# A two-layer recurrent decoder trunk: moving the small tiles so that the large ones start on multiples of 256 bytes

## The chip, the cores and the metric

The kernel runs on one core of a Trainium2 chip. The metric is the time of one execution on the device in microseconds (us), as the median of several runs; less is better. TensorE (PE in the profile) multiplies matrices, VectorE (DVE), ScalarE (ACT) and GpSimd (POOL) work elementwise, and SyncE (SP) issues all of this kernel's transfers. The on-chip memory has 128 partitions; a tile takes the same range of byte addresses in each of them, and that range is what this change moves.

## What is computed

The input x has 512 tokens of 2048 float32 values. Two layers and a last norm follow:

```
x = x + lru_mlstm_layer(rmsnorm(x, e_norm), ...)     # layer 0
x = x + ssd_layer(rmsnorm(x, o_norm), ...)           # layer 1
return rmsnorm(x, final_norm)

def lru_mlstm_layer(x, w_in, ...):
    u = x @ w_in                                     # 2048 -> 8192
    x_l, x_m, z = split(u)
    y_l = rglru(causal_conv(x_l), ...)               # gated linear recurrence
    q, k, v, o = projections of conv(x_m) and x_m    # 4 heads
    y_m = o * rmsnorm(mlstm_chunkwise(q, k, v, gates))
    return (concat(y_l, y_m) * silu(z)) @ w_out      # 4096 -> 2048

def ssd_layer(x, w_in, ...):
    z, xbc, dt = split(x @ w_in)                     # 2048 -> 10304
    y = ssd_scan(silu(causal_conv(xbc)), softplus(dt + dt_bias), ...)
    return rmsnorm_by_group(y * silu(z)) @ w_out     # 4096 -> 2048
```

All arrays are float32. About nine tenths of the arithmetic is the four large products with `w_in` and `w_out`.

## The kernel before

Everything lies transposed: channels on the partitions, the 512 tokens along the free dimension. A float32 product is made of three products in a faster format (`fp32r` in the profile): a value is split into a high and a low part, and `mm3` (lines 136 to 140) issues high by high (L138), high weight by low activation (L139) and low weight by high activation (L140). Each is a 128x128 weight tile (the stationary operand, loaded by LDWEIGHTS, `PEld` in the profile) against a 128x512 activation tile (the moving operand).

- `acc` holds the running x, 16 tiles of 128x512. `prenorm` writes its two parts, multiplied by the norm's weights, into `xh[0..15]` and `xl[0..15]`. Every input projection of both layers (`proj`) has these as its moving operands: in the profile `xm`, `zm`, `xl`, `zl`, `xbc`, `z` and `dt` name the results, and the operands read `xh,whi`, `xl,whi` and `xh,wlo`.
- `load_w` brings weights: one DMA of 128x1024 into `wraw` (2 buffers), then per half a copy on ACT into `whi` (L131) and a subtraction on DVE into `wlo` (L132), 4 buffers each. Its instructions are recorded with a high priority.
- `outproj` multiplies a group's result by `w_out` and adds to `acc` (L207). Its moving operands are the working tiles `yh`, `yl` (also `ylh`, `yll`, `ymh`, `yml`); only for the last head of layer 0 and half of the last group of layer 1 do they lie in the space of `xh` and `xl`, which is free then.
- The mixers' other work (convolution, gates, attention, scan) is cut into stages, generators that `tick` moves on after a number of weight chunks, so that it fills in beside the projections. In the attention the moving operands `Ph`, `Pl` meet the stationary `vh`, `vl` (result `num`).
- At the end the 16 column tiles of the last output projection are done in two halves of 256 tokens; there the weights lie in `xh` and `xl`, as stationary operands.

The order on each engine comes from the recording order and priorities; a scheduler sets it when the program is built. The address of a tile is set by the pools: pools are stacked in the order in which they are opened, and a tile takes its bytes per partition, rounded up to 32. `prm`, the array of small parameters, is the first tile of the first pool, 872 columns or 3488 bytes, and starts 128 bytes behind a multiple of 256. Before the change the pool `cst` has behind it `eps` and `warm` (4 bytes each), `ones_r` (512), `r_bc` (2048), `acc` (32768), `xh` and `xl` (2048 each), and `raws` (2 tiles of 2060 bytes); then comes the pool `wp` with `wraw`, `whi` and `wlo`. So the distance of each start behind a multiple of 256 bytes is:

```
                          before   after
prm                         128     128
ones_r                       96       0
r_bc, acc, xh, xl            96       0
wraw, whi, wlo              160       0
raw0, raw1                96, 128   0, 32
working tiles of both
layers (yh, yl, Ph, vh,
xs, Bt, Bn, ...)            224      64
```

The working tiles' pools lie behind those of the table's first rows, and all their tiles but a few small ones are multiples of 256 bytes long, so one number holds for nearly all. Every start is a multiple of 32 before and after.

Of the kernel before, what the change touches and what calls it, by code (L numbers as in the profile page):

```python
# [9 lines left out]
F32 = mybir.dt.float32  # L10
F32R = mybir.dt.float32r
# [5 lines left out]
P = 128  # L17
# [6 lines left out]

# columns of the packed per-partition parameter array
_W = [
# [12 lines left out]
NPAR = _o  # L39
# how many weight chunks pass before each stage of the mixers' work  # L40
LAG = dict(P=6, rs=2, late=3, dtr=15, CB=5, xtr=6, st=4, yo=1, att_rs=4, vtr=2, aitr=12, num=7, pr=2)
# where the column tiles of the previous group's output projection go in
VB = (2, 2)
# [4 lines left out]
def trunk(ctx, tc, x_t, par, w_in0, w_qkvo, w_lru, w_if, w_out0, w_in1, w_out1, out):  # L48
# [4 lines left out]
    cst = ctx.enter_context(tc.tile_pool(name="cst", bufs=1))  # L53
    wp = ctx.enter_context(tc.tile_pool(name="wp", bufs=1))
    pmm = ctx.enter_context(tc.tile_pool(name="pmm", bufs=3, space=PSUM))
# [9 lines left out]
    def pc(name, j=0, n=1):  # L65
        o = OFF[name][0] + j
        return prm[:, o:o + n]
# [4 lines left out]
    v.memset(eps, EPS)  # L72
    warm = cst.tile([P, 1], F32, name="warm")
    sc.activation(warm, eps, AF.Square)
    ones_r = cst.tile([P, P], F32R, name="ones_r")
    ones = ones_r.bitcast(F32)
    r_bc = cst.tile([P, S], F32, name="r_bc")
# [4 lines left out]
    xpairs = list(zip(xh, xl))  # L82
    raws = [cst.tile([P, S + 3], F32, name=f"raw{i}") for i in range(2)]
    for t in raws:
# [6 lines left out]

# [1 line left out]
    gens = []  # L93
# [20 lines left out]

# [1 line left out]
    def load_w(src, dsts=(None, None), pieces=1, ahead=3000):  # L116
# [24 lines left out]

    # one chunk: four contraction tiles, from the k-th on, of n
    def chunk(ps, w, mov, k, n):
# [22 lines left out]

    # in pieces: a reciprocal is slow, and the weights' splits go in between
    def recip(dst, src, w=S):
        for o in range(0, w, P):
            v.reciprocal(dst[:, o:o + P], src[:, o:o + P])  # L170

    # dst = 1 / sqrt(ssq / n + eps) on all partitions; ssq: per-partition partial sums
    def rstd(dst, ssq, n):
# [9 lines left out]

    # log1p(e) for 0 <= e <= 1 as 2 atanh(e / (2 + e))
    def log1p(dst, e, t1, t2):
        v.tensor_scalar(t1, e, 2.0, None, op0=ADD)
        v.reciprocal(t1, t1)
        v.tensor_tensor(t1, e, t1, op=MUL)
        v.tensor_tensor(t2, t1, t1, op=MUL)
        v.tensor_scalar(dst, t2, 1.0 / 15, 1.0 / 13, op0=MUL, op1=ADD)  # L190
        for c in (11, 9, 7, 5, 3, 1):
            v.tensor_tensor(dst, dst, t2, op=MUL)
            v.tensor_scalar(dst, dst, 1.0 / c, None, op0=ADD)
        v.scalar_tensor_tensor(dst, t1, 2.0, dst, op0=MUL, op1=MUL)

    # softplus(s * x) for s = +-1
    def softplus(dst, x, s, t0, t1, t2):
        v.scalar_tensor_tensor(t0, x, -1.0, x, op0=MUL, op1=MAX)
        sc.activation(t0, t0, AF.Exp, scale=-1.0)
        log1p(dst, t0, t1, t2)  # L200
        v.tensor_scalar(t0, x, s, 0.0, op0=MUL, op1=MAX)
        v.tensor_tensor(dst, dst, t0, op=ADD)

    # out of PSUM, ahead of other work: the tensor engine needs the bank
    def evac(o, a, b, op):
        with tc.high_priority(offset=1000):
            v.tensor_tensor(o, a, b, op=op)  # L207

    # causal convolution of a padded tile (bias included)
    def conv(dst, raw, w, b):  # L210
# [3 lines left out]

    # the two parts of acc * norm
    def prenorm(k, norm):
# [9 lines left out]

    # acc += w_out[rows of group g].T @ y, some column tiles
    def outproj(w_out, g, ys, js, done=None):
# [9 lines left out]

    # ================= layer 0 =================
    qd = [dr.tile([2, P, S], F32, name=f"qd{h}") for h in range(NH)]  # L240
# [10 lines left out]

    nlam = L0.tile([P, 16], F32, name="nlam")
    aiT = L0.tile([P, 16], F32, name="aiT")
    ln = [L0.tile([P, 16], F32, name=f"ln{i}") for i in range(3)]

# [29 lines left out]

# [1 line left out]
    pA = tc.tile_pool(name="A", bufs=1)  # L287
# [6 lines left out]

    # four contraction tiles at a time, in the four column strips of the array
    def gate_mm(kt, rhs):
# [4 lines left out]

    # the first two column tiles go along with the loads of x
    ps01 = [mmt("xm"), mmt("xm")]
# [6 lines left out]
    for h in range(NH):  # L310
        xm, xc = [], []
        for t in range(4):
            j = 4 * h + t
            if j > 1:
                ps = mmt("xm")
                proj(ps, w_in0[16 + j], xpairs)
            else:
                ps = ps01[j]
            if j == 0:
                v.tensor_tensor(ssq0[0], ssq0[0], ssq0[1], op=ADD)  # L320
                spawn(rstd(r_bc, ssq0[0], D))
                drain()
            raw = next_raw()
            evac(raw[:, 3:], ps, r_bc, MUL)
            m = xslot("xm")
            split(m[0], m[1], raw[:, 3:])
            xm.append(m)
            a = st("ca")
            conv(a, raw, pc("cm_w", 4 * j, 4), pc("cm_b", j))
            s = st("cs")  # L330
            sc.activation(s, a, AF.Sigmoid)
            v.tensor_tensor(a, a, s, op=MUL)
            c = xslot("xc")
            split(c[0], c[1], a)
            xc.append(c)
            tick()
            if j == 0:
                # -8 softplus(-lam)
                softplus(nlam, pc("lam", 0, 16), -1.0, *ln)
                v.tensor_scalar(nlam, nlam, -8.0, None, op0=MUL)  # L340
# [64 lines left out]

    # gates of all heads: ai = i - G, M = max(0, cummax ai), exp(-m) = exp(-(G + M))
    ready = []

    def gates():
        g_s = st("gs")  # L410
        sc.copy(g_s, ps_g)
        yield 1
        pg = axt("pg")
        pe.matmul(pg[0:36], pc("gsel", 0, 36), g_s, start=True, stop=True)
        g_i, g_f, g_t0, g_t1, g_t2 = [st(f"g{i}")[0:4] for i in range(5)]
        g_G = st("gG")[0:4]
        v.tensor_scalar(g_i, pg[0:4], pc("b_i")[0:4], None, op0=ADD)
        sc.copy(g_f, pg[32:36])
        v.tensor_scalar(g_f, g_f, pc("b_f")[0:4], None, op0=ADD)
        softplus(g_G, g_f, -1.0, g_t0, g_t1, g_t2)  # L420
        for c in range(4):
            cs = slice(c * P, (c + 1) * P)
            v.tensor_tensor_scan(g_t0[:, cs], ones[0:4], g_G[:, cs],
                                 0.0 if c == 0 else g_t0[:, c * P - 1:c * P], op0=MUL, op1=ADD)
        # g_t0 = -G
        v.tensor_tensor(g_i, g_i, g_t0, op=ADD)
        v.tensor_tensor_scan(g_t1, g_i, g_i, 0.0, op0=MAX, op1=MAX)
        v.tensor_tensor(g_t2, g_t0, g_t1, op=SUB)
        sc.activation(g_t2, g_t2, AF.Exp)
        dma(md[0:NH], g_t1)  # L430
        dma(md[NH:2 * NH], g_t2)
        ready.append(True)
        yield LAG["aitr"]
        pt = axt("aitr")
        for s in range(4):
            pe.transpose(pt[:, 4 * s:4 * s + 4], g_i[:, s * P:(s + 1) * P], ident[0:4, 0:4])
        sc.copy(aiT, pt[:, 0:16])
        ready.append(True)

# [1 line left out]
    def lru_tile(j, out_y):  # L441
# [46 lines left out]

# [1 line left out]
    def attention(h, yl, out_y):  # L490
# [115 lines left out]

    # ================= layer 1 =================
    dad = dr.tile([64, S], F32, name="dad")
    ed = dr.tile([64, S], F32, name="ed")
    dcd = dr.tile([64, 2], F32, name="dcd")  # L610

# [1 line left out]
    ps = mmt("dt")  # L613
# [8 lines left out]
    def lt(tag, bufs=1, shape=(P, S), dt=F32):  # L622
        return L1.tile(list(shape), dt, tag=tag, name=tag, bufs=bufs)

    dasT, dtT, dwT = [lt(n, shape=(P, 4, 64)) for n in ("dasT", "dtT", "dwT")]
    dcb = lt("dcb", shape=(P, 64, 2))
    na = lt("na", shape=(P, 1))[0:64]
    dc = lt("dc", shape=(P, 2))[0:64]

# [29 lines left out]

    # input projection, convolution and silu of one channel tile of x | B | C  # L660
    def xbc(j, dst):
# [27 lines left out]
    def pair(G, t, xs):  # L689
# [33 lines left out]
        yield LAG["st"]  # L723
        # states at the chunk boundaries
        pst = axt("st")
# [5 lines left out]
        for c in (1, 2):  # L731
# [3 lines left out]
            v.tensor_tensor(Sx[:, c], Sx[:, c], pst[:, c * P:(c + 1) * P], op=ADD)  # L735
        # within the chunks
        pd = axt("yd")
# [5 lines left out]
        yield LAG["yo"]  # L743
        # from the states
        po = axt("yo")
# [75 lines left out]

# [1 line left out]
    wl = []  # L823
# [39 lines left out]

# column tiles, contraction chunks of 8 tiles, each [128, 8 * 128] and contiguous
def _wpack(w):
# [4 lines left out]

# pairs of column tiles, contraction chunks of 4 tiles
def _wpair(w):
# [73 lines left out]
```

## Time and profile before

| | us |
|---|---|
| median of 3 runs | 2709.31 (2709.21 to 2709.97) |
| span of the profiled execution, first to last instruction | 2708.4 |
| PE busy | 2680.3 |
| VectorE busy | 1729.7 |
| ScalarE busy | 1191.2 |
| DMA queue's share of 16 engines | 34.1% |

The profiled execution's own time is not listed beside its span; the three runs are 0.8 to 1.6 us longer than that span, which is what lies around it. The durations of matmuls in the profile overlap: one that lasts 0.39 us is followed by the next after some 0.23 us.

### The profile page before, as it was taken

To read this page: it belongs to the slowest core of one execution; us is meant where nothing else is said; L and a number is where in the kernel's file an instruction comes from. 1 tells how busy PE (TensorE), PEld (TensorE's weight loads), DVE (VectorE), ACT (ScalarE), POOL (GpSimd) and SP (SyncE) were. 2 spreads that over 40 slices of the span, in tenths; PEclk is the share of its full clock that TensorE was granted. 3 is DMA by queue.
4 is the path that set the end of the run, shared out by engine and by line. 5 is a ranking of instruction groups with operands and counts; after the bars stand their busy time and mean duration, and the time that the engine had idled before them with its cause. 6 is when DMAs were issued, how large, how long until landed. Compare 5 with 4: busy or idle time off the path is not lost.

```text
span 2708.4 us, 33237 instructions
## 1 busy us (share of the span) xinstructions
PE 2680.3 (99%) x12462; PEld 2176.9 (80%) x12462; DVE 1729.7 (64%) x2940; ACT 1191.2 (44%) x1882; POOL 118.5 (4%) x116
## 2 busy tenths in 40 slices
PE   8999999999999999999999999999999999999997
PEld 6778778777888888888888888888888888888887
DVE  8453535387757657665786667656677566675666
ACT  6343333356436436453555343443434434344445
POOL 1000000000000000000200000000000000000004
PEclk9999999999999999999999999999999999999999
DMA  4334342433333333323243332323324233242332
GB/s 164 115 112 135 98 139 90 157 100 122 114 107 105 114 103 107 103 90 99 96 126 109 109 109 94 124 94 109 109 89 130 94 106 111 87 125 95 107 98 101
DMA packets 114385, 297.74 MB, mean 110 GB/s; under 512 B 11688, under 2 KB 34472, under 8 KB 114224
## 3 DMA queue, kind: packets, MB, share of 16 engines
q1 hardware_dynamic: 114224, 295.62, 34.1%
q8 instruction: 98, 1.61, 0.2%
q14 instruction: 63, 0.52, 0.1%
HBM read 278.52 MB, written 17.06 MB: 109 GB/s over the span
## 4 chain that ended last, share of the span: by engine, by line
PE 96%; DVE 3%; DMA 1%; issue 0%; ACT 0%; POOL 0%; SPq 0%; DVEq 0%; ACTq 0%; POOLq 0%
PE po L140 8%; PE po L139 8%; PE po L138 8%; PE xbc L138 7%; PE xbc L140 7%; PE xbc L139 7%; PE z L138 4%; PE z L139 4%; PE z L140 4%; PE xl L138 2%; PE xm L138 2%; PE xm L140 2%; PE xl L139 2%; PE zm L140 2%; PE zm L139 2%; PE xl L140 2%
## 5 line engine op out<-in xcount | busy, mean ns | idle before, releaser
L131 ACT CAST whi<-wraw 128x512 fp32r<-128x512 f32 x886 | 545.7, 616 | 1211.6 <-PE po L139 255.4
L132 DVE TENSOR_TENSOR wlo<-wraw,whi 128x512 fp32r<-128x512 f32 x886 | 609.9, 689 | 467.1 <-ACT whi L131 434.0
L138 PE MATMUL xbc<-xh,whi 128*128 128x512 f32 x768 | 306.8, 399 | 0.0
L139 PE MATMUL xbc<-xl,whi 128*128 128x512 f32 x768 | 303.6, 395 | 0.0
L140 PE MATMUL xbc<-xh,wlo 128*128 128x512 f32 x768 | 303.6, 395 | 0.0
L207 DVE TENSOR_TENSOR acc<-acc,po 128x512 f32<-128x512 f32 (+1 forms) x272 | 176.5, 651 | 172.4 <-PE po L140 171.8
L138 PE MATMUL z<-xh,whi 128*128 128x512 f32 x512 | 205.0, 400 | 0.0
L139 PE MATMUL z<-xl,whi 128*128 128x512 f32 x512 | 202.4, 395 | 0.0
L140 PE MATMUL z<-xh,wlo 128*128 128x512 f32 x512 | 202.3, 395 | 0.0
L138 PE MATMUL po<-yh,whi 128*128 128x512 f32 (+1 forms) x456 | 179.8, 394 | 0.0
L140 PE MATMUL po<-yh,wlo 128*128 128x512 f32 (+1 forms) x456 | 178.6, 392 | 0.0
L139 PE MATMUL po<-yl,whi 128*128 128x512 f32 (+1 forms) x456 | 177.5, 389 | 0.0
L140 PEld LDWEIGHTS xbc<-xh,wlo 128*128 128x128 f32 x768 | 144.4, 188 | 34.9
L138 PEld LDWEIGHTS xbc<-xh,whi 128*128 128x128 f32 x768 | 144.4, 188 | 34.4 <-issue 1.2
L139 PEld LDWEIGHTS xbc<-xl,whi 128*128 128x128 f32 x768 | 144.5, 188 | 33.2
L225 POOL TENSOR_TENSOR ssq<-ssq,sq 128x512 f32<-128x512 f32 (+1 forms) x79 | 89.2, 1129 | 1685.7 <-ACT sq L224 1684.9
L140 PEld LDWEIGHTS z<-xh,wlo 128*128 128x128 f32 x512 | 96.3, 188 | 23.3
L138 PEld LDWEIGHTS z<-xh,whi 128*128 128x128 f32 x512 | 96.3, 188 | 22.0 <-issue 0.2
L139 PEld LDWEIGHTS z<-xl,whi 128*128 128x128 f32 x512 | 96.4, 188 | 21.9
L138 PE MATMUL xm<-xh,whi 128*128 128x512 f32 x256 | 104.1, 407 | 6.5 <-ACT whi L131 5.9
L140 PE MATMUL xm<-xh,wlo 128*128 128x512 f32 x256 | 103.2, 404 | 3.0 <-DVE wlo L132 3.0
L139 PE MATMUL xm<-xl,whi 128*128 128x512 f32 x256 | 103.7, 405 | 0.0
(339 smaller groups left out, 5425.9 us busy)
## 6 DMA issues: line engine op xcount, KB each, us to landing
wraw<-in_w_in_dram SPq DMA_DIRECT2D x288, 512.0 KB, 3.3
wraw<-in_w_out_dram SPq DMA_DIRECT2D x128, 512.0 KB, 3.3
dab<-dad SPq DMA_DIRECT2D x64, 256.0 KB, 3.6
wraw<-in_w_qkvo_dram SPq DMA_DIRECT2D x24, 512.0 KB, 3.3
E<-ed SPq DMA_DIRECT2D x64, 128.0 KB, 3.2
vd<-vn SPq DMA_DIRECT2D x16, 256.0 KB, 3.5
od<-zm SPq DMA_DIRECT2D x16, 256.0 KB, 3.3
V<-vd SPq DMA_DIRECT2D x16, 256.0 KB, 3.8
```

Source lines behind the costliest of these rows:

```text
L131: sc.copy(hi[:, :m], raw[:, i:i + m])
L132: v.tensor_tensor(lo[:, :m], raw[:, i:i + m], hi[:, :m].bitcast(F32), op=SUB)
L138: pe.matmul(ps, wh, mh, start=first, stop=False)
L139: pe.matmul(ps, wh, ml, start=False, stop=False)
L140: pe.matmul(ps, wl, mh, start=False, stop=last)
L207: v.tensor_tensor(o, a, b, op=op)
L225: eng.tensor_tensor(ssq, ssq, sq, op=ADD)
```

## The change

The tiles of `cst` are put in another order, and the pools in another stack. Behind `prm` now come only small tiles: `eps`, `nlam`, `aiT` (both from the layer-0 pool), `na` and `dc` (both from the layer-1 pool). Their rounded sizes, 32, 64, 64, 32 and 32 bytes, bring the next tile to a multiple of 256. `ones_r` and `raws` go into a new pool `cst2` behind the weight buffers. `warm` is gone; the first activation, which loads ACT's table, writes into `nlam`. The three scratch tiles `ln` of 128x16 are gone; the softplus of the recurrence's parameter takes them from the ring of working tiles `st` (6 buffers of 128x512), three of which it holds meanwhile. The rest of the diff removes comments.

```
     cst = ctx.enter_context(tc.tile_pool(name="cst", bufs=1))
-    wp = ctx.enter_context(tc.tile_pool(name="wp", bufs=1))
...
-    warm = cst.tile([P, 1], F32, name="warm")
-    sc.activation(warm, eps, AF.Square)
-    ones_r = cst.tile([P, P], F32R, name="ones_r")
-    ones = ones_r.bitcast(F32)
+    nlam = cst.tile([P, 16], F32, name="nlam")
+    aiT = cst.tile([P, 16], F32, name="aiT")
+    sc.activation(nlam[:, 0:1], eps, AF.Square)
+    na = cst.tile([P, 1], F32, name="na")[0:64]
+    dc = cst.tile([P, 2], F32, name="dc")[0:64]
     r_bc = cst.tile([P, S], F32, name="r_bc")
     acc_t = cst.tile([P, KD, S], F32, name="acc")
...
-    raws = [cst.tile([P, S + 3], F32, name=f"raw{i}") for i in range(2)]
+    wp = ctx.enter_context(tc.tile_pool(name="wp", bufs=1))
+    cst2 = ctx.enter_context(tc.tile_pool(name="cst2", bufs=1))
+    ones_r = cst2.tile([P, P], F32R, name="ones_r")
+    ones = ones_r.bitcast(F32)
+    raws = [cst2.tile([P, S + 3], F32, name=f"raw{i}") for i in range(2)]
...
-    nlam = L0.tile([P, 16], F32, name="nlam")
-    aiT = L0.tile([P, 16], F32, name="aiT")
-    ln = [L0.tile([P, 16], F32, name=f"ln{i}") for i in range(3)]
...
-                softplus(nlam, pc("lam", 0, 16), -1.0, *ln)
+                softplus(nlam, pc("lam", 0, 16), -1.0, *[st("ln")[:, :16] for _ in range(3)])
...
-    na = lt("na", shape=(P, 1))[0:64]
-    dc = lt("dc", shape=(P, 2))[0:64]
```

No large tile changes its size, and PE's instructions stand in the same order before and after. On the other engines the order moves at two places. The first is VectorE near the program's start, where the sum of squares of x (`ssq`) is finished; `ln` and `nlam` are the softplus of 128x16. Before:

```order
L225 TENSOR_TENSOR ssq_227<-ssq_227,sq 128x512
L198 SCALAR_TENSOR_TENSOR ln_138<-prm 128x16
L225 TENSOR_TENSOR ssq_227<-ssq_227,sq 128x512
L132 TENSOR_TENSOR wlo<-wraw,whi 128x512
L186 TENSOR_SCALAR ln_139<-ln_138 128x16
L187 RECIPROCAL ln_139<-ln_139 128x16
L320 TENSOR_TENSOR ssq_227<-ssq_227,ssq0b 128x512
L188 TENSOR_TENSOR ln_139<-ln_138,ln_139 128x16
```

After, at the same place (line numbers are about 5 higher, `L636` is the negation of the state decay `na`, whose inputs were there all along):

```order
L230 TENSOR_TENSOR ssq_228<-ssq_228,sq 128x512 x2
L137 TENSOR_TENSOR wlo<-wraw,whi 128x512
L636 TENSOR_SCALAR na<-na 64x1
L322 TENSOR_TENSOR ssq_228<-ssq_228,ssq0b 128x512
L164 TENSOR_TENSOR rl<-ssq_228,rh 128x512
L137 TENSOR_TENSOR wlo<-wraw,whi 128x512
L175 RECIPROCAL r_bc<-std 128x128
```

And some 13 rows later on VectorE, among the convolutions (`ca`) of the first channel tiles, after the change:

```order
L212 TENSOR_TENSOR raw_119<-xm,r_bc 128x512
L203 SCALAR_TENSOR_TENSOR ln<-prm 128x16
L334 TENSOR_TENSOR ca<-ca,cs 128x512
L137 TENSOR_TENSOR wlo<-wraw,whi 128x512
L191 TENSOR_SCALAR ln<-ln 128x16
L192 RECIPROCAL ln<-ln 128x16
```

The 22 small instructions of the softplus moved from the chain that ends in `r_bc` to behind it, and `na` came forward from layer 1. The second place is the DMA queue (SP) at the start of layer 1, where the time steps' sums (`dad`), their exponentials (`ed`) and chunk decays (`dcd`) go out and come back as broadcasts (`dab`, `E`, `dcb`). Before:

```order
L61 DMA dad<-xs 64x512
L61 DMA ed<-xs 64x512
L61 DMA dcd<-dc 64x2
L61 DMA dab<-dad 128x512 x2
L123 DMA wraw<-in_w_in_dram 128x1024
L61 DMA dcb<-dcd 128x128
L61 DMA E<-ed 64x512 x2
```

After:

```order
L60 DMA dad<-xs 64x512
L60 DMA dab<-dad 128x512 x2
L128 DMA wraw<-in_w_in_dram 128x1024
L60 DMA ed<-xs 64x512
L60 DMA dcd<-dc 64x2
L60 DMA dab<-dad 128x512
L60 DMA E<-ed 64x512
L60 DMA dcb<-dcd 128x128
L60 DMA E<-ed 64x512
```

Two broadcasts and one load of weights now stand ahead of `ed` and `dcd`.

## The prediction

> **What bounds the kernel now.** I read the page first, then the busy time by stage. Of the page: the span, PE's busy time, and the chain of work that ended last, by engine.
>
> ```profile
> span 2708.4 us, 33237 instructions
> PE 2680.3 (99%) x12462; PEld 2176.9 (80%) x12462; DVE 1729.7 (64%) x2940; ACT 1191.2 (44%) x1882; POOL 118.5 (4%) x116
> PE 96%; DVE 3%; DMA 1%; issue 0%; ACT 0%; POOL 0%; SPq 0%; DVEq 0%; ACTq 0%; POOLq 0%
> ```
>
> PE is the bound. The windows on PE alone (start:end, length, busy time, instructions, granted clock, DMA share, GB/s) say where its idle time lies:
>
> ```profile
> 0.00:67.00 67.00, 56.95 (x213) 0.95 0.48 165
> 67.00:2600.00 2533.00, 2530.56 (x11669) 1.00 0.34 109
> 2600.00:2694.00 94.00, 91.59 (x579) 1.00 0.29 96
> 2694.00:2709.00 15.00, 1.20 (x4) 0.60 0.41 140
> ```
>
> From 67 to 2600 us PE idles 2.4 us in all, at full clock: no wait can be shortened there by more. The rest idles 10.1, 2.4 and 13.8 us. So a change that moves no multiplication and takes none away can matter in two ways: in the head and the tail, or through how fast one matmul follows another. I looked at the second more closely, in two stretches in which nothing but 128x512 matmuls runs and PE is never idle. First the two windows, then what runs in each (the first has `xh`, `xl` as moving operands, the second the working tiles `ylh`, `yll`; behind the bar are busy us and mean ns of one):
>
> ```profile
> 160.00:230.00 70.00, 70.00 (x302) 1.00 0.28 91
> 1273.00:1315.00 42.00, 42.00 (x185) 1.00 0.31 101
> ```
>
> ```profile
> L138 PE MATMUL zm<-xh,whi 128*128 128x512 f32 x59 | 23.3, 396 | 0.0
> ```
>
> ```profile
> L138 PE MATMUL po<-ylh,whi 128*128 128x512 f32 x62 | 24.1, 388 | 0.0
> ```
>
> 302 instructions touch 70 us, and the first and last stick out by one duration, so one follows another every (70 + 0.396) / 302 = 233.1 ns; in the second stretch every (42 + 0.391) / 185 = 229.1 ns. The same instruction, of the same size and at the same clock, is 4 ns slower when it streams `xh` and `xl`. The durations show the same by group:
>
> ```profile
> L139 PE MATMUL xbc<-xl,whi 128*128 128x512 f32 x768 | 303.6, 395 | 0.0
> L139 PE MATMUL z<-xl,whi 128*128 128x512 f32 x512 | 202.4, 395 | 0.0
> L140 PE MATMUL xm<-xh,wlo 128*128 128x512 f32 x256 | 103.2, 404 | 3.0 <-DVE wlo L132 3.0
> L138 PE MATMUL zm<-xh,whi 128*128 128x512 f32 x256 | 101.2, 396 | 0.0
> L139 PE MATMUL zm<-xl,whi 128*128 128x512 f32 x256 | 101.2, 396 | 0.0
> L140 PE MATMUL zm<-xh,wlo 128*128 128x512 f32 x256 | 101.2, 396 | 0.0
> L139 PE MATMUL xl<-xl,whi 128*128 128x512 f32 x256 | 101.3, 396 | 0.0
> L139 PE MATMUL zl<-xl,whi 128*128 128x512 f32 x256 | 101.2, 395 | 0.0
> L138 PE MATMUL po<-xh,whi 128*128 128x512 f32 x64 | 25.3, 395 | 0.0
> L140 PE MATMUL po<-ymh,wlo 128*128 128x512 f32 x192 | 75.6, 394 | 0.0
> L139 PE MATMUL po<-yml,whi 128*128 128x512 f32 x192 | 75.3, 392 | 0.0
> L138 PE MATMUL po<-ymh,whi 128*128 128x512 f32 x192 | 74.5, 388 | 0.0
> L140 PE MATMUL num<-Ph,vl 128*128 128x512 f32 x16 | 6.3, 395 | 0.0
> L138 PE MATMUL num<-Ph,vh 128*128 128x512 f32 x16 | 6.3, 394 | 0.0
> L139 PE MATMUL num<-Pl,vh 128*128 128x512 f32 x16 | 6.3, 393 | 0.0
> ```
>
> Groups that stream `xh` and `xl` take 395 to 396 ns (`xm` is longer because it runs partly in the head, at a lower clock); `ymh`, `yml` 391.3 in the mean. It isn't the code: `po<-xh` is the output projection, as `po<-ymh` is, and takes 395, only because its data lies in `xh`. What differs is the address. `xh` starts 96 bytes behind a multiple of 256, `whi` 160: the stream starts 64 bytes short of the weights (modulo 256). The y tiles start at 224, 64 bytes past the weights. In `num` both operands start at 224, distance 0: 394.0 in the mean. So the spacing hangs on where the two operands start; which property of the addresses decides isn't in the trace.
>
> **The change part by part.** *The addresses of x and the weights.* The moving `xh`, `xl` meet `whi`, `wlo` 3 x (768 + 512 + 4 x 256 + 64) = 7104 times at 512 columns. Before, the distance is -64, afterwards 0. The only group of this size in the trace that has distance 0 is `num`, at 394.0 against 395.5 for the x groups (between the 395 and 396 of the rows). If the distance decides, that is -1.5 ns x 7104 = -10.7 us. All of it lies on the path, since PE is busy throughout. The bounds: down to the 391.3 of the y groups, -4.2 x 7104 = -29.8 us; up to the slow half of the x group's own durations, which alternate between two values:
>
> ```profile
> L138 PE MATMUL zm<-xh,whi x256: 393/396/398, 62.6 to 486.9; 128*128 128x512 f32 x128
> ```
>
> 398 for all would be +2.5 x 7104 = +17.8 us. I take the value of `num`, the one row with the new distance, although it has 48 instances, broken by shorter matmuls.
>
> *The y tiles* go from 224 to 64 while the weights go from 160 to 0: the distance stays 64, so I price them at 0. `ones_r` and the stationary x of the last stage are few instructions; 0 as well.
>
> *The transfers.* The DMA targets `acc` and `wraw` get aligned. The DMA queue's row of the page, and whom the queue waited for:
>
> ```profile
> q1 hardware_dynamic: 114224, 295.62, 34.1%
> ```
>
> ```profile
> SPq L123 <- DVE wlo L132: 1941.6, 424, 7.7
> ```
>
> The engines are used to a third, and the loads of weights stand 1941.6 us waiting for a free buffer: a faster transfer only waits longer behind it. The Trainium skill (DMA: Bandwidth & Descriptors, How a descriptor splits into AXI transactions) says that a descriptor which doesn't start on 256 bytes begins at the boundary below and pays for the bytes between; by that, estimated, a 4096-byte row that starts 160 behind costs 133 beats instead of 128, 4% less after the change, and none of it is on this path. In the head transfers can be waited for; the waits of its first 45 us that concern PE and x:
>
> ```profile
> PE xm L138 <- ACT whi L131: 5.9, 1, 5.9
> ACT xh L217 <- DMA acc<-in_x_t_dram: 3.4, 3, 1.8
> PE xm L140 <- DVE wlo L132: 3.0, 1, 3.0
> ```
>
> 5.9 us is the start itself, 3.0 us is VectorE, and 3.4 us is all that ACT waited for x. So the transfers' gain lies between 0 and 3.4 us; I take 0.3, a tenth of it, since the rows of x would have to be far faster to take more.
>
> *The softplus that moves on VectorE.* Its dearest row and its typical one, and the window of all engines behind it (PE, PEld, DVE, ACT, POOL):
>
> ```profile
> L198 DVE SCALAR_TENSOR_TENSOR ln<-prm x1: 1261/1261/1261, 35.0 to 35.0; 128x16 f32<-128x16 f32 x1
> L192 DVE TENSOR_TENSOR nlam<-nlam,ln x6: 169/176/176, 40.0 to 43.1; 128x16 f32<-128x16 f32 x6
> ```
>
> ```profile
> 40.00:67.00 27.00, 26.88 (x115) 21.70 (x116) 24.31 (x49) 15.14 (x24) 0.00 (x0) 1.00 0.30 96
> ```
>
> 22 instructions, some 21 x 0.18 + 1.26 = 5.0 us, leave the way to `r_bc` and go between the first convolutions, ahead of `wlo` and of the copies out of PSUM. PE is busy 26.88 of 27 us while they run now, so taking them away gives nothing there. Put in later, they hold DVE up by 5 us where a projection of 48 matmuls lasts 48 x 0.233 = 11.2 us and three banks take turns; the cover is a bank's time, and it holds. Cost 0; without that cover, 5.0 us. `warm` and `na`, one instruction each, cost nothing.
>
> *The DMA queue at layer 1.* `ed` and `dcd` are now issued behind two broadcasts and a load of weights that may wait up to 7.7 us for its buffer (the row of SP's waits). The chunk decays' way back and their first use:
>
> ```profile
> L732 DVE TENSOR_TENSOR Sx<-Sx,dcb x64: 278/284/294, 1390.6 to 2591.6; 128x128 f32<-128x128 f32 x64
> L61 SPq DMA_DIRECT2D dcb<-dcd x1: 320/320/320, 1371.9 to 1371.9; - x1
> ```
>
> Issued at 1371.9 and used at 1390.6: 18.7 us of room for at most some 9 us of delay. Cost 0.
>
> *Sum.* -10.7 - 0.3 = -11.0 us against the profiled execution. Its span is 2708.4; the runs are 0.8 to 1.6 us above that, which the change doesn't touch. So 2709.3 - 11.0 = 2698.3 us.
>
> **The rivals.** A measurement of this kernel can tell about 0.2% from no change, 5.4 us.
>
> *No change, 2709 us.* What decides is something that the change keeps: a class of distances (0 and -64 alike), or the region of memory, which shifts by less than 5 KB. For it: in `num` the rows of 393 to 395 overlap with the 395 of the x groups, and its 512-column matmuls are too few to show a steady state. The spacing of x stays at 233.1 +- 0.7 ns, and the time within 0.2%. The Trainium skill speaks for this too (SBUF — State Buffer, Specifications): it gives lines of 16 bytes, and every start here was a multiple of 32 before. The traces' 4 ns between two such starts speak against that rule as the whole of it.
>
> *The alignment itself helps, all streams.* The other groups of the y stream, beside `ymh`, for their counts:
>
> ```profile
> L138 PE MATMUL po<-yh,whi 128*128 128x512 f32 x448 | 177.5, 396 | 0.0
> L138 PE MATMUL po<-ylh,whi 128*128 128x512 f32 x256 | 101.0, 395 | 0.0
> ```
>
> If what costs is the start inside a 64-byte block (all of 96, 160 and 224 are 32 past one, and 0 and 64 are not), every matmul could come down to the fastest row, 388: -7.5 x 7104 - 3.3 x 3 x (448 + 256 + 192) = -53.3 - 8.9 = -62 us, 2647 us. Against it: the trace has no 512-column matmul of either kind of start to show it.
>
> *Slower: equal starts collide.* If stream and weight load use the same part of memory when both start at 0, each x matmul takes the slow 398: +17.8 us, 2727 us. It decides from a mean duration of 396.3 ns up (5.4 us / 7104 = 0.8 ns above 395.5). For it: distance 0 in `num` is slower than distance 64 by 2.7 ns. Against it: `num` is still faster than x is now.
>
> *Slower by the ring of working tiles.* Three of the six `st` buffers are held by `ln` meanwhile; if the first convolutions wait for them longer than the banks cover, the 5.0 us show: 2714 to 2716 us.
>
> **How the numbers follow.** Forecast 0.35, no change 0.32, alignment for all 0.12, collision 0.17, ring 0.04. The two first are nearly even; I put the forecast ahead because a row of the trace prices it. Faster 0.35 + 0.12 = 0.47, same 0.32, slower 0.17 + 0.04 = 0.21. The forecast's own range is 2679 (y's pace) to 2704. The range of all reaches from 2665, which leaves out most of the case at 2647, to 2728, just above the collision.
>
> **What would show it.** Right: the mean durations of `zm`, `xl`, `zl` near 394, the window of pure x matmuls at about 231.6 ns, the y groups at 391.3 as before, PE still idle only in head and tail. Wrong: x groups unmoved at 395.5 (no change), at 398 (collision), y groups moved (the distance is not what decides), or a window between 40 and 70 us in which PE waits for VectorE (ring).

## The result, and the profile after

The change takes the median from 2709.26 us (2708.61 to 2709.97, 4 runs) to 2669.03 us (2667.21 to 2669.74, 4 runs), a ratio of 0.9849 with a 95% interval of 0.9837 to 0.9861: 40.2 us less. The forecast was 11 us less.

The page of the profiled execution (2669.7 us, span 2668.0): span, busy time, the chain that ended last, the DMA queue.

```profile
span 2668.0 us, 33237 instructions
PE 2639.6 (99%) x12462; PEld 2175.2 (82%) x12462; DVE 1727.9 (65%) x2940; ACT 1194.3 (45%) x1884; POOL 118.3 (4%) x116
PE 94%; DVE 3%; DMA 1%; issue 0%; ACT 0%; POOL 0%; DVEq 0%; ACTq 0%; POOLq 0%
q1 hardware_dynamic: 114224, 295.62, 33.5%
```

PE has the same 12462 matmuls and is busy 2680.3 - 2639.6 = 40.7 us less; the span is 2708.4 - 2668.0 = 40.4 us shorter. So nothing was won from waits. The windows of PE say the same (start:end, length, busy, instructions, granted clock, DMA share, GB/s):

```profile
0.00:67.00 67.00, 56.89 (x215) 0.95 0.46 166
67.00:2560.00 2493.00, 2489.89 (x11668) 1.00 0.34 111
2560.00:2655.00 95.00, 92.68 (x583) 1.00 0.28 95
2655.00:2668.00 13.00, 0.10 (x1) 0.55 0.46 161
```

Idle time is 10.1, 3.1, 2.3 and 12.9 us, 28.4 in all, where it was 28.1. What changed is the pace. First the window of 70 us in which only `xh` and `xl` are streamed, then the groups (operands; behind the bar busy us and mean ns of one; the lines of `mm3` are now 143 to 145):

```profile
160.00:230.00 70.00, 70.00 (x310) 1.00 0.29 98
```

```profile
L144 PE MATMUL xbc<-xl,whi 128*128 128x512 f32 x768 | 298.9, 389 | 0.0
L144 PE MATMUL z<-xl,whi 128*128 128x512 f32 x512 | 199.3, 389 | 0.0
L145 PE MATMUL xm<-xh,wlo 128*128 128x512 f32 x256 | 101.8, 399 | 2.9 <-DVE wlo L137 2.9
L143 PE MATMUL zm<-xh,whi 128*128 128x512 f32 x256 | 99.6, 389 | 0.0
L144 PE MATMUL zm<-xl,whi 128*128 128x512 f32 x256 | 99.6, 389 | 0.0
L145 PE MATMUL zm<-xh,wlo 128*128 128x512 f32 x256 | 99.6, 389 | 0.0
L144 PE MATMUL xl<-xl,whi 128*128 128x512 f32 x256 | 99.7, 390 | 0.0
L144 PE MATMUL zl<-xl,whi 128*128 128x512 f32 x256 | 99.6, 389 | 0.0
L143 PE MATMUL po<-xh,whi 128*128 128x512 f32 x64 | 24.9, 389 | 0.0
L145 PE MATMUL po<-ymh,wlo 128*128 128x512 f32 x192 | 75.3, 392 | 0.0
L144 PE MATMUL po<-yml,whi 128*128 128x512 f32 x192 | 74.5, 388 | 0.0
L143 PE MATMUL po<-ymh,whi 128*128 128x512 f32 x192 | 75.7, 394 | 0.0
L145 PE MATMUL num<-Ph,vl 128*128 128x512 f32 x16 | 6.3, 394 | 0.0
L144 PE MATMUL num<-Pl,vh 128*128 128x512 f32 x16 | 6.3, 393 | 0.0
L143 PE MATMUL num<-Ph,vh 128*128 128x512 f32 x16 | 6.2, 389 | 0.0
```

310 matmuls touch the 70 us where 302 did: one every (70 + 0.389) / 310 = 227.1 ns instead of 233.1 (231.6 were forecast). Every x group shown fell by 4 to 6 ns, `zm` from 395.3 to 389.1 (its busy time by its count). Added up over the rows of all x groups of 512 columns, the 6384 matmuls outside `xm` fell from 396.5 to 390.8 ns in the mean and the 768 of `xm` from 404.9 to 399.7: 36.7 us and 4.0 us by their rows, 40.7 us, which is the whole difference. The three groups with `ymh` and `yml` stand at 391.3 in the mean, as before, and all y groups at 393.0; only which of the three has which value changed.

### The profile page after: what moved, and what is told of

It reads as the page before. It is cut to its first block, busy times and chain, and to the rows that moved or that the text cites. A ratio compares the mean times of both kernels' runs of the same rounds, so it can differ in the third digit from the quotient of the medians.

```text
span 2668.0 us, 33237 instructions
## 1 busy us (share of the span) xinstructions
PE 2639.6 (99%) x12462; PEld 2175.2 (82%) x12462; DVE 1727.9 (65%) x2940; ACT 1194.3 (45%) x1884; POOL 118.3 (4%) x116
## 3 DMA queue, kind: packets, MB, share of 16 engines
q1 hardware_dynamic: 114224, 295.62, 33.5%
## 4 chain that ended last, share of the span: by engine, by line
PE 94%; DVE 3%; DMA 1%; issue 0%; ACT 0%; POOL 0%; DVEq 0%; ACTq 0%; POOLq 0%
PE po L143 8%; PE po L145 8%; PE po L144 8%; PE xbc L143 7%; PE xbc L145 7%; PE xbc L144 7%; PE z L143 4%; PE z L145 4%; PE z L144 4%; PE xl L143 2%; PE xl L145 2%; PE xl L144 2%; PE zm L143 2%; PE zm L145 2%; PE zm L144 2%; PE zl L145 2%
```

## The experiments

All of them change only where tiles lie, and PE's idle time (span less busy time) stays between 26 and 31 us in every one, so what they differ by is the pace of the matmuls. "Distance" is the start of the moving operand minus the start of its weights, modulo 256 bytes. Means over all y groups go by their 2688 matmuls of 512 columns.

**Is it the distance, or the multiple of 256?** Four kernels.

Kernel `b_raws_behind` is the kernel before with one edit, which moves the weights and nothing else:

```
     wp = ctx.enter_context(tc.tile_pool(name="wp", bufs=1))
+    cst2 = ctx.enter_context(tc.tile_pool(name="cst2", bufs=1))
...
-    raws = [cst.tile([P, S + 3], F32, name=f"raw{i}") for i in range(2)]
+    raws = [cst2.tile([P, S + 3], F32, name=f"raw{i}") for i in range(2)]
```

> The kernel before with one edit: the two padded tiles raw0 and raw1 (2060 bytes each, 2080 with the rounding) move from ahead of the weight buffers to behind them. x's two parts stay at 96 mod 256, the weights move from 160 to 96, the layers' tiles (y among them) stay at 224. No small tile is gathered, softplus keeps its three tiles. So x and its weights start alike without being on a multiple of 64 or 256. Theory D (the pace depends on the distance of the moving operand's start from the weights' start, mod 256): the x groups fall from 395.5 to the 389 to 390 ns of the kernel after, some 6 ns on 7104 matmuls, -41 us: 2668; the y streams go from a distance of +64 to +128, which no run has shown, between 227 and 233 ns each, -5 to +11 us: 2663 to 2680. Theory A (a start on a multiple of 64 or 256 is what helps, of x or of the weights): 96 is none, so 2709 and x at 395.5. Theory O (the other edits of the change, softplus's tiles and the transfers, brought it): 2709.

Measured: 2678.72 us, ratio to the kernel before 0.9885 (0.9871 to 0.9900). Its window of pure x matmuls, and its groups:

```profile
160.00:230.00 70.00, 70.00 (x310) 1.00 0.30 98
```

```profile
L139 PE MATMUL zm<-xh,whi 128*128 128x512 f32 x256 | 99.7, 389 | 0.0
L139 PE MATMUL po<-ymh,whi 128*128 128x512 f32 x192 | 75.9, 395 | 0.0
```

x and the weights both start at 96, which is no multiple of 64, and x has the whole gain: 227.1 ns. With theory A and theory O that can't be. The y streams, now at a distance of 128, went from 391.3 to 395 in `ymh`, and from 393.0 to 396.3 in the mean of all y groups: 8.9 of the 9.7 us by which this kernel is slower than the one after.

Kernel `a_x0_w64` goes the other way: x stays on a multiple of 256, and only the weights are shifted, by taking the `raws` from `cst2` into a pool `mid` that is opened ahead of `wp`:

```
+    mid = ctx.enter_context(tc.tile_pool(name="mid", bufs=1))
     wp = ctx.enter_context(tc.tile_pool(name="wp", bufs=1))
...
-    raws = [cst2.tile([P, S + 3], F32, name=f"raw{i}") for i in range(2)]
+    raws = [mid.tile([P, S + 3], F32, name=f"raw{i}") for i in range(2)]
```

> The kernel after with the two padded tiles raw0 and raw1 ahead of the weight buffers again: x stays at 0 mod 256, the weights move from 0 to 64, the layers' tiles stay at 64. Distance of x -64 as in the kernel before, of y 0. Theory D: x back at 395.5 ns, +41 us, and the y streams at 0 instead of +64, about 2 ns less on some 2700 matmuls, -5 us: 2704, y groups from 391.3 to 389. Theory A with x's start (0 mod 256) as what helps: 2669; A with the weights on a multiple of 256: 2709; on a multiple of 64: 2669. Theory O: 2669.

Measured: 2704.39 us, 0.9982 (0.9973 to 0.9991). Its groups:

```profile
L144 PE MATMUL zm<-xh,whi 128*128 128x512 f32 x256 | 101.3, 396 | 0.0
...
L144 PE MATMUL po<-ymh,whi 128*128 128x512 f32 x192 | 74.8, 389 | 0.0
```

All of the change's other edits are in this kernel, x starts on a multiple of 256, and 35.4 of the 40 us are gone again. What is left of the gain lies in the y streams, which have distance 0 here: their mean fell from 393.0 to 391.4, 4.3 us, and 2709.7 - 4.3 = 2705.4 against 2704.4 measured. So the softplus, `na` and the transfers' order are worth nothing that can be seen. Of the targets of the transfers only `acc` starts on a multiple of 256 here, `wraw` doesn't; what both are worth together is seen further below, where everything starts at 0 (2659.7 us) or at 64 (2661.6 us): at most some 2 us, and the two ratios' intervals overlap.

Kernel `a_x64_w0` puts the four small tiles between x and the weights, so that x has the +64 that y has in the kernels before and after. `mid` is opened behind `cst` and ahead of `wp`, as above; then

```
-    nlam = cst.tile([P, 16], F32, name="nlam")
-    aiT = cst.tile([P, 16], F32, name="aiT")
+    nlam = mid.tile([P, 16], F32, name="nlam")
+    aiT = mid.tile([P, 16], F32, name="aiT")
...
-    na = cst.tile([P, 1], F32, name="na")[0:64]
-    dc = cst.tile([P, 2], F32, name="dc")[0:64]
+    na = mid.tile([P, 1], F32, name="na")[0:64]
+    dc = mid.tile([P, 2], F32, name="dc")[0:64]
```

> The kernel after with the four small tiles between x and the weight buffers: x at 64 mod 256, the weights at 0, the layers' tiles at 64. Distance of x +64, as y has it in both kernels. Theory D: x at y's 391.3 ns, 2 ns more than after on 7104 matmuls, +15 us: 2684, y unchanged. Theory A: with multiples of 64, or with the weights on 256, 2669; with x on 256, 2709. Theory O: 2669.

Measured: 2681.90 us, 0.9896 (0.9880 to 0.9913). Its window, and the three groups of `zm`:

```profile
160.00:230.00 70.00, 70.00 (x307) 1.00 0.29 98
```

```profile
L146 PE MATMUL zm<-xh,wlo 128*128 128x512 f32 x256 | 100.8, 394 | 0.0
...
L145 PE MATMUL zm<-xl,whi 128*128 128x512 f32 x256 | 100.1, 391 | 0.0
...
L144 PE MATMUL zm<-xh,whi 128*128 128x512 f32 x256 | 99.8, 390 | 0.0
```

(70 + 0.392) / 307 = 229.3 ns, the 229.1 of the y streams before: x takes y's pace at y's distance. The measured 12.9 us above the kernel after stand against the 15 expected.

Kernel `a_all_0` sets everything to 0: the `raws` go ahead of `r_bc`, `na` and `dc` into a small pool at layer 1's end, which moves the layers' tiles from 64 to 0:

```
+    raws = [cst.tile([P, S + 3], F32, name=f"raw{i}") for i in range(2)]
     r_bc = cst.tile([P, S], F32, name="r_bc")
...
     L1 = ctx.enter_context(tc.tile_pool(name="L1", bufs=1))
+    L1b = ctx.enter_context(tc.tile_pool(name="L1b", bufs=1))
...
+    dc = L1b.tile([P, 2], F32, name="dc")[0:64]
+    na = L1b.tile([P, 1], F32, name="na")[0:64]
```

> The kernel after with na and dc in a pool of layer 1 at its end and the padded tiles raw0 and raw1 ahead of r_bc: x, the weights and the layers' tiles with y among them all at 0 mod 256. Theory D: x as after (389 to 390), the y streams at distance 0 instead of +64, 2 ns less on some 2700 matmuls: -5 us, 2664, y groups at 389. Theory A with multiples of 64: 2669; with 256: some us less through y, 2664. Theory O: 2669.

Measured: 2659.71 us (2658.70 to 2660.43, 4 runs), 0.9816 (0.9802 to 0.9831): faster than the kernels before and after, 9.3 us below the latter. Its groups:

```profile
L141 PE MATMUL zm<-xh,whi 128*128 128x512 f32 x256 | 99.7, 389 | 0.0
...
L141 PE MATMUL po<-ymh,whi 128*128 128x512 f32 x192 | 74.7, 389 | 0.0
L143 PE MATMUL num<-Ph,vl 128*128 128x512 f32 x16 | 6.2, 389 | 0.0
```

y joined x at 389. Over all y groups the mean fell from 393.0 to 391.1, some 5 us, as expected. The other 4 us were not expected. About 1 us of them lies ahead of 67 us, by when 219 matmuls had run instead of 215; the granted clock of the first 40 us was 0.96 instead of 0.91, and that the change of address is behind that was not shown. The rest is open.

**Which distances are slow?** Six kernels with x and y both at 64 and the weights alone shifted. The edit is that of `a_x64_w0`, with fewer or more of the small tiles in `mid`, ahead of the weights, and the others in `cst2`, behind them. The one for 128:

```
-    nlam = cst.tile([P, 16], F32, name="nlam")
-    aiT = cst.tile([P, 16], F32, name="aiT")
+    nlam = mid.tile([P, 16], F32, name="nlam")
+    aiT = mid.tile([P, 16], F32, name="aiT")
...
-    na = cst.tile([P, 1], F32, name="na")[0:64]
-    dc = cst.tile([P, 2], F32, name="dc")[0:64]
+    na = cst2.tile([P, 1], F32, name="na")[0:64]
+    dc = cst2.tile([P, 2], F32, name="dc")[0:64]
```

Ahead of the weights lie: none for 0; `nlam`, `aiT`, `na`, `dc` and `raw0` for +32; `nlam`, `aiT` and `na` for +96; `nlam` and `na` for -96; `na` for -32.

> The kernel after with nlam, aiT, na and dc behind the weight buffers instead of ahead of r_bc: x, the weights and the layers' tiles with y all start at 64 mod 256, distance 0, none on a multiple of 256. Theory D (only the distance counts): as with all of them at 0, 2660, x and y at 389 to 390. Theory A (0 mod 256 is itself worth something): between 2660 and the 2669 of after, with x above 389.

> The kernel after with nlam, aiT, na, dc and raw0 between x and the weight buffers: x and y at 64, the weights at 32 mod 256, distance +32 for both. Theory D with a cost that grows step by step: between 0 and +64 (389 and 391.3), about 390, 2671. Theory D with a step at every distance but 0 and +64: 395.5, 2720. Theory B (blocks of 64 bytes; 32 lies in the block below 64, so it acts as +64): 391.3, 2682.

> The kernel after with nlam, aiT and na between x and the weight buffers and dc behind these: x and y at 64, the weights at 224 mod 256, distance +96 for both (64 + 256 - 224). Theory D with a cost that grows step by step: between +64 and 128 (391.3 and 395), about 393, 2700. With a step: 395.5, 2720. Theory B (blocks of 64; 224 lies in the block at 192, so it acts as 128): 395, 2719.

> The kernel after with nlam and aiT between x and the weight buffers, na and dc behind these: x at 64, the weights at 192, the layers' tiles at 64 mod 256, so x and y both at the distance 128 (-128 is the same mod 256). Theory D, with y's 128 in the kernel before with the padded tiles behind (its y groups took 395 ns): x and y at 395, 2660 + 6 ns x 9888 matmuls = 2719. Rival R2 (128 is alike with 0, since a period of 128 would do): 2660. Rival y (the 395 of y there was not from the distance but from the neighbouring x streams): x and y below 395, 2680 to 2700.

> The kernel after with nlam and na between x and the weight buffers and aiT and dc behind these: x and y at 64, the weights at 160 mod 256, distance -96 for both. Theory D in every form: between 128 (395) and -64 (395.5), so 395, 2719. Theory with a period of 64 in which a distance off the multiples of 64 costs more: above 395.5, over 2720.

> The kernel after with na between x and the weight buffers and nlam, aiT and dc behind these: x and y at 64, the weights at 96 mod 256, distance -32 for both, which no run has shown. Theory D with a cost that grows step by step around 256 (0: 389, +64: 391.3, 128: 395, -64: 395.5): -32 lies between -64 and 0, about 392, 2690. Theory D with a step (every distance but 0 and +64 costs all): 395.5, 2720. Theory B (what counts is the block of 64 bytes, 64 and 96 are in one): 389, 2660.

The runs measured this, with `a_x64_w0` as the series' +64 and with -64 from `a_x0_w64` (whose y is at 0, so its time is not comparable). The spacing is (70 us + one duration) by the count in the window from 160 to 230 us; one instruction more or less is 0.8 ns:

```
distance  count  spacing   zm (ns)       us       ratio to before (95%)
   0       311   226.3     389           2661.64  0.9824 (0.9808 to 0.9841)
 +32       302   233.1     395           2722.17  1.0042 (1.0019 to 1.0065)
 +64       307   229.3     390/391/394   2681.90  0.9896 (0.9880 to 0.9913)
 +96       301   233.9     395/397/392   2723.58  1.0051 (1.0028 to 1.0074)
 128       303   232.3     395           2715.76  1.0025 (1.0014 to 1.0035)
 -96       300   234.7     396           2732.98  1.0080 (1.0057 to 1.0103)
 -64       301   233.9     396           -        -
 -32       301   233.9     396           2723.21  1.0052 (1.0032 to 1.0072)
```

The scatter of one or two counts is mostly the window's edge. From the first start to the last in the same window, read off the timeline of PE, one matmul follows another every 226.7 ns at distance 0 (in all four kernels with x at 0, 64 or 96), 228.9 at +64, 232.4 at 128, 234.3 at -96 and 233.3 at the other four distances, in the kernel before (-64) too.

The windows at distance 0, +32, 128 and -96:

```profile
160.00:230.00 70.00, 70.00 (x311) 1.00 0.29 98
```

```profile
160.00:230.00 70.00, 70.00 (x302) 1.00 0.27 90
```

```profile
160.00:230.00 70.00, 70.00 (x303) 1.00 0.28 92
```

```profile
160.00:230.00 70.00, 70.00 (x300) 1.00 0.27 90
```

And two groups of the kernel at -32:

```profile
L144 PE MATMUL zm<-xh,whi 128*128 128x512 f32 x256 | 101.3, 396 | 0.0
L144 PE MATMUL po<-ymh,whi 128*128 128x512 f32 x192 | 75.9, 396 | 0.0
```

A step, not a slope, as the second form of theory D had it (2720 for +32, +96 and -32): distance 0 is fast wherever the operands start (at 0, at 64, and x at 96), +64 lies near it, and all the others are at 232 to 235 ns. My form with a cost that grows step by step missed +32 (2671 expected, 2722 measured), +96 (2700, 2724) and -32 (2690, 2723). Theory D missed -96 in every form (2719 expected, 2733 measured): its pace is 1 ns slower than that of the others, and why is open. The blocks of 64 bytes (theory B) fall with +32 (2682 expected) and with -32, where 64 and 96 lie in one block and the pace is slow. A period of 128 falls with 128, and so does the thought that y's 395 in `b_raws_behind` came from its neighbours (2680 to 2700 expected, 2716 measured). From 0 to -96 the same work takes 71 us more, 2.7%. In the kernel with everything at 64, x and its weights agree in their starts modulo 512 (a weight tile is a slice of 512 bytes) and `ymh` and its weights only modulo 256; both take 389, so 256 is enough.

A rival that moves with the weights would be the engines that write them: ScalarE and VectorE fill `whi` and `wlo` at the very addresses that were shifted. The timeline rules it out. Between 160 and 230 us each three matmuls in a row take 0.70 us from start to start in the kernel before and in the one at -32, and 0.68 us in the kernel after, in all of some 100 threes each, a third of which run while no weight part is written.

**Whose weights are they?** A matmul streams while the weights of the next are loaded: in the kernel before, the load for the matmul on `xh,whi` that starts at 180.25 us runs from 180.02 us for 0.19 us, and the matmul ahead of it from 180.02 us for 0.40 us. Two kernels set only one of the two kinds of weights to 64, with a pool `wpl` for `wlo` behind `wp` (`a_wlo64`) or ahead of it (`a_whi64`), and the `raws` between:

```
-                    lo = wp.tile([P, 512], F32R, tag="wlo", name="wlo", bufs=4)
+                    lo = wpl.tile([P, 512], F32R, tag="wlo", name="wlo", bufs=4)
```

> The kernel after with the padded tiles and the low parts of the weights in pools behind whi's: x and whi at 0, wlo and y at 64 mod 256. A matmul streams x while the weights of the next one are loaded. The order is (xh, whi), (xl, whi), (xh, wlo). Theory D-own (the distance of the moving operand from its own matmul's weights): of x only the third matmul, (xh, wlo), is at -64, a third of 7104 by 6 ns: +14 us; of y the third is at 0 instead of +64, -2 us: 2681, with the group of zm on xh,wlo near 395 and the two on whi at 389 to 390. Theory D-next (from the weights that are loaded while it streams, those of the matmul behind it): the same sum, but the slow one is the second, (xl, whi), which streams x while wlo is loaded: zm on xl,whi near 395, the other two at 389 to 390. Theory where three in a row must agree for the fast pace: all three near 395, 2704.

Measured: 2696.69 us, 0.9953 (0.9937 to 0.9969).

```profile
L147 PE MATMUL zm<-xh,wlo 128*128 128x512 f32 x256 | 101.7, 397 | 0.0
L146 PE MATMUL zm<-xl,whi 128*128 128x512 f32 x256 | 100.4, 392 | 0.0
L145 PE MATMUL zm<-xh,whi 128*128 128x512 f32 x256 | 99.6, 389 | 0.0
```

> The mirror of the kernel with wlo alone at 64: the low parts of the weights and x at 0, the high parts with wraw at 64, y at 64 mod 256. Of the three matmuls (xh, whi), (xl, whi), (xh, wlo) the first two are at distance -64, the third at 0. That run gave 397, 392 and 389 ns for (xh, wlo), (xl, whi), (xh, whi) of zm, and 28 us more than after where a third of the x groups' 41 us were expected. Theory D-own (the own weights' distance decides): the two on whi near 396, (xh, wlo) near 389 to 391; two thirds of 41 us, 2696. Theory D-change (what costs is that the weights' start changes from one matmul to the next, twice in three in both kernels): the same 28 us as that run had, 2697, with the slow group the one whose weights differ from those ahead of them on the other side, (xh, wlo) and (xh, whi). Theory D-all (the fast pace needs the whole row of three at distance 0): 2704 and over, all three at 395.

Measured: 2710.05 us, 1.0006 (0.9994 to 1.0017).

```profile
L146 PE MATMUL zl<-xl,whi 128*128 128x512 f32 x256 | 101.2, 395 | 0.0
L147 PE MATMUL zl<-xh,wlo 128*128 128x512 f32 x256 | 101.2, 395 | 0.0
...
L147 PE MATMUL zm<-xh,wlo 128*128 128x512 f32 x256 | 101.2, 396 | 0.0
...
L146 PE MATMUL zm<-xl,whi 128*128 128x512 f32 x256 | 101.0, 394 | 0.0
...
L145 PE MATMUL zm<-xh,whi 128*128 128x512 f32 x256 | 100.7, 393 | 0.0
```

With the third at -64 the slowest group is that third, as D-own has it, but its neighbour loses too, and the time is 28 us above the kernel after instead of 12. With two thirds at -64 the remaining third, at distance 0, is not fast: on `xh,wlo` `zl` takes 395 and `zm` 396, the slowest of its three, and 41 us are back, some 4 of them in the y streams (393.0 to 394.5 in the mean, 2688 matmuls). So a matmul's own distance isn't all of it, and none of the theories put forward (own, next, change, all) gives both runs. Which read meets which stays open. What they do show: to get the whole gain, all the weights of the run must start like the stream.

## Why the prediction was right or wrong

**The bound** was right. From 67 us to 2694 us before and to 2655 us after, PE idles some 5 us in all, and the 40 us lie in its busy time.

**The addresses of x and the weights** is the step that failed, by its size. "If the distance decides" was right, as `b_raws_behind` and `a_x0_w64` show. The price was not: "I take the value of `num`, the one row with the new distance" gave -1.5 ns and -10.7 us, and the x groups fell by 6.2 ns in `zm` and by 40.7 us in all. `num` was no measure of distance 0. Its operands start alike in all of these kernels, and its three rows stood at 395, 394 and 393 before, at 394, 393 and 389 after, and at 389 in `a_all_0`. The prediction named the weakness, 48 instances "broken by shorter matmuls", and took the row all the same. Why the row differs from kernel to kernel at one distance was not shown. Its bounds were no bounds either: y's 391.3 as the lower end supposed that distance 0 can't be faster than +64, and the row for that was `num` again. The slow half of the durations at the upper end, "398 for all", belonged to distance -64, where 393 and 398 alternate; it says nothing of another distance. The reading of the x groups was rough too, though little hangs on it: the groups on `xh,whi` of `xbc`, `z` and `zl` stood at 399, 400 and 403, not at 395 to 396, and they fell by 5 to 6 ns with the others.

**The y tiles** at 0 were right: 391.3 in the three `ymh` and `yml` groups before and after, at the same distance, although both operands moved. That they could be had too, by 64 bytes more, I didn't see; that is some 5 of the 9 us of `a_all_0`.

**The transfers** at 0.3 us were right in that nothing came of them. The waits of the first 45 us:

```profile
PE xm L143 <- ACT whi L136: 5.8, 1, 5.8
...
ACT xh L222 <- DMA acc<-in_x_t_dram: 3.4, 3, 1.8
PE xm L145 <- DVE wlo L137: 2.9, 1, 2.9
```

ACT waits 3.4 us for x, as before; the queue's share went from 34.1 to 33.5%, 923.6 to 893.8 us of the span on the mean engine. `a_x0_w64` has the share lower still, 33.1%, at 35 us more, so the share is no cause.

**The softplus and the queue at layer 1** at 0 were right. The chunk decays:

```profile
L732 DVE TENSOR_TENSOR Sx<-Sx,dcb x64: 277/284/293, 1371.2 to 2551.9; 128x128 f32<-128x128 f32 x64
L60 SPq DMA_DIRECT2D dcb<-dcd x1: 1481/1481/1481, 1357.7 to 1357.7; - x1
```

They are issued 13.5 us ahead of their first use instead of 18.7, so 5 of the room of 18.7 us were used up and nobody waits.

**The rivals.** *No change* falls with the interval. The Trainium skill gives lines of 16 bytes (SBUF — State Buffer, Specifications). The series shows that they don't describe this: all starts are multiples of 32, and the pace runs from 226 to 235 ns. *The alignment itself* falls with the y groups, which the change put from 32 past a block of 64 onto one without moving them, with x at 96 in `b_raws_behind` (fast), and with `d_128`, where all starts are multiples of 64 (slow). *The collision of equal starts* has the sign reversed: it is unequal starts that cost. Its support, distance 0 slower than +64, was the row of `num` once more. *The ring of working tiles* falls with PE's waits between 40 and 67 us, of which the profile after names one, 0.7 us for `rh` (0.6 before). The chances gave 0.47 to faster, mainly on this mechanism; the forecast's own range ended at 2679, and the measured 2669 lies inside the wide one only because that took in part of the rival at 2647.

## What to carry to other kernels

Where matmuls with a weight load each run back to back, let the moving operand and all the weights that it meets start at the same byte modulo 256; which byte did not matter here (0, 64 and, for x, 96), and 32 bytes of a small tile between two pools cost 2.3% of the time here (2661.6 to 2723.2 us). Look for it by the spacing: count the matmuls in a window in which PE is never idle, for one operand and then for another. And when a row is the only one with the new condition, ask whether it shows a steady state before it carries the price, and leave the side open on which no row lies.

## What the runs showed of the hardware that was not expected

- The pace of a 128x512 matmul in this format, at full granted clock, is 226 to 227 ns when stream and weights start alike modulo 256, 229 at +64, and 232 to 235 at the other distances in steps of 32, with no slope between them.
- +64 and -64 differ (229.3 and 233.9 ns), so it isn't the size of the distance.
- The loads of the weights themselves don't show it; the rows of `zm` on `xh,whi` in the kernel before and then after have the same 188 ns:

```profile
L138 PEld LDWEIGHTS zm<-xh,whi 128*128 128x128 f32 x256 | 48.1, 188 | 11.6
```

```profile
L143 PEld LDWEIGHTS zm<-xh,whi 128*128 128x128 f32 x256 | 48.1, 188 | 9.9
```

- The Trainium skill (TensorE: Matmul & The Clock Gate, Step-by-step: what each phase is for) gives PE two independent read ports, one for the stream and one for the weights. The series shows the pace hanging on the starts of both together, which speaks against two reads that leave each other alone; where they meet was not shown.
